# Attention of blocks 4 to 7 in two pairs, each beside merge, selection and gates of the pair ahead

## The chip, the core and the metric

One core of a Trainium2 chip runs the whole program. The metric is device time in microseconds of one execution; three runs of the kernel before gave 3388.62, 3393.28 and 3394.96, median 3393.28. All numbers are float32 unless said otherwise. The engines are TensorE (PE), VectorE (DVE), ScalarE (ACT), GpSimd (POOL) and the queue of SyncE (SP), which issues most of the transfers.

## What is computed

The reference is one layer on 1024 tokens of width 1024:

```
proj = rmsnorm(x, w1) @ w_in                     # 8 groups of columns: q, k, v of two attentions, two gates
o_d  = differential attention, 8 heads, softmax(q1 k1) - lam * softmax(q2 k2), causal by chunks of 64
o_c  = chunk attention, 8 heads, each chunk of 64 sees itself and 8 chunks to the left
h    = x + (sig(g_d) * (o_d @ w_bd) + sig(g_c) * (o_c @ w_bc)) @ w_out
q    = rmsnorm(h, w2) @ wq                       # 8 heads x 2 halves, 128 keys each
       top 16 of each half, top 16 of the 256 sums -> 8 x 16 experts of 16384 per token, weights by softmax
h    = h + sum over the chosen experts  gelu(u[e] . xn) * g * v[e]
y    = rmsnorm(h, final_norm_w)
```

## The kernel before

The tokens are eight blocks of 128. Two ways serve the experts. Blocks 2 to 5 (`DBLK`) go through all 16384 experts as dense matmuls in 128 chunks (`dense_experts`, L681), with the chosen weights laid out as a gate table; blocks 0, 1, 6, 7 (`SBLK`) gather each chosen row by indirect DMA (`experts`, L789): per block 128 gathers from u with a product on VectorE each (L809), then 128 from v with a sum each (L815). Blocks 0 and 1 form projection group 0, blocks 2 to 7 group 1.

The steps around the change are generators that `weave` (L52) runs in turn, so that their instructions are written alternately:

- `attention` (L304): for each of 8 heads and each block the scores of the two maps (L347), a VectorE pass that adds the bias and takes the minimum (L353), exp on ScalarE (L360), the combination of the two maps (L392), transposes, copies and products with V (L366 to L373). Then 4 head pairs of the chunk attention. K, V and Q of a head are loaded when its first block comes (`kv_load`, L311). `diff_end` (L408) writes the reciprocal norms of the heads to DRAM.
- `merge` (L478) of a pair of blocks: the norms come back as a broadcast of 1 MB (L495), then branch products, output product, second norm, query product and the first top 16 (`top16`, L558).
- `choose` (L565), called by `sel`: the second top 16, the expert numbers (through one-hot tiles `ohib`) and the softmax weights of one block. For a dense block it leaves the transposed numbers and weights in `it4` (L629).
- `gates` (L643): for four tokens at a time two one-hot tiles (`o2` on VectorE, L653; `o1` half on ScalarE, L660 and L661, half on VectorE, L663), four small products (L669) and a copy into the staging tile `gst` (L671). After 32 tokens `gst`, 2 MB, is stored to DRAM (L673). A block takes 32 steps.

Before, blocks 4 to 7 went through one attention (`att_rest`, L838), beside merge and selection of blocks 2 and 3. Its outputs were stored to DRAM per head (`ond`, `ocd`) and loaded again per pair (`mop`, L848). Then merge 4, 5 ran beside the gates of blocks 2, 3, and merge 6, 7 beside selection 4, 5 and, after that, the gates of 4, 5. Selection 6, 7 and the dense experts follow, and last in the source stand the gathers.

The order on each engine is laid out when the program is built: a planner walks through the instructions by the order in which they were written and by when its model of their costs says that their inputs are ready, so that what was written late fills gaps. Each engine then runs its list strictly in order. A tile whose place in SBUF belonged to an earlier tile waits until that one is released. Pools are opened and closed as a stack: what `at2` held is free for `gk` only afterwards. The split of a weight tile into two parts (`wtile`, L192; `split`, L126) uses the tags `wh` and `wl` of the pool `wp`, which stands for the whole program.

Of the kernel before, what the change touches and what calls it, by code (L numbers as in the profile page):

```python
# [7 lines left out]
F32 = mybir.dt.float32  # L8
F32R = mybir.dt.float32r
# [6 lines left out]
P = 128  # L16
# [24 lines left out]
JG = 4  # L41
PBUFS = 4
LAG = 1
GLAG = 2
GACT = 2
W1N = 46
HALVES = (slice(0, 64), slice(64, 128))
# [19 lines left out]
def chain(*gens):  # L67
    for g in gens:
        yield from g
# [3 lines left out]
def layer_kernel(ctx, tc, x, w1, w_in, b_gate, lq1, lk1, lq2, lk2, subln, rel,  # L73
# [23 lines left out]
    hd = [drp.tile([P, D], F32, name=f"hd{b}") for b in range(NB)]  # L97
    gdr = [drp.tile([P, NCH, TB], F32, name=f"gdr{i}") for i in range(DT // TB)]
    rst = {}
    ond = [drp.tile([P, 4 * P], F32, name=f"ond{h}") for h in range(H)]  # L100
    ocd = [drp.tile([P, 4 * P], F32, name=f"ocd{h}") for h in range(4)]

    cst = con.tile([P, 3], F32, name="cst")
    for i, c in enumerate((EPS, -0.5 * EPS, 1.5)):
# [46 lines left out]
    def setup():  # L151
# [37 lines left out]
        nc.sync.dma_start(nbias, bass.AP(tensor=tfd.tensor, offset=tfd.offset + 127, ap=[[383, P], [P * 384, H], [1, 256]]))  # L189
        nc.vector.memset(nbias[0:64, :, 192:256], BIG)  # L190

    def wtile(src, K=KC):  # L192
        raw = wp.tile([P, KC, P], F32, name="wr", tag="wr", bufs=WBUFS)[:, :K, :]
        nc.sync.dma_start(raw, src)
        hi = wp.tile([P, KC, P], F32R, name="wh", tag="wh")[:, :K, :]
        lo = wp.tile([P, KC, P], F32R, name="wl", tag="wl")[:, :K, :]
        split(raw, hi, lo)
        return hi, lo

# [12 lines left out]
    def norm1(gi, xp):  # L212

        T = len(GROUPS[gi]) * P
        xh = xp.tile([P, KC, T], F32R, name="xh", tag="xh")
        xl = xp.tile([P, KC, T], F32R, name="xl", tag="xl")
        for i, b in enumerate(GROUPS[gi]):
            xt = wp.tile([P, KC, P], F32, name="xt", tag="wr", bufs=WBUFS).rearrange("p a b -> p (a b)")
            nc.sync.dma_start(xt, x[b * P:(b + 1) * P, :])
            xs = wp.tile([P, KC, P], F32, name="xs", tag="wl").rearrange("p a b -> p (a b)")  # L220
            ss = sm.tile([P, 1], F32, name="ss", tag="ss")
            nc.scalar.activation(xs, xt, AF.Square, accum_out=ss)
            r = rsqrt(sm, ss, 1, 1.0 / D)
            nc.scalar.activation(xs, xt, AF.Copy, scale=r)
            for g in range(2):
                o = transposes([xs[:, (4 * g + j) * P:(4 * g + j + 1) * P] for j in range(4)])
                for j in range(4):
                    c = 4 * g + j
                    oj = o[:, j * P:(j + 1) * P]
                    hi, lo = xh[:, c, i * P:(i + 1) * P], xl[:, c, i * P:(i + 1) * P]  # L230
                    nc.scalar.activation(hi, oj, AF.Copy, scale=w1c[:, c:c + 1])
                    nc.vector.scalar_tensor_tensor(lo, oj, w1c[:, c:c + 1], hi.bitcast(F32), op0=OP.mult, op1=OP.subtract)  # L232
            yield
        dn[gi].x = (xh, xl)
# [330 lines left out]
    def choose(yz, b):  # L565
# [60 lines left out]
        nc.vector.reciprocal(gs, gs)  # L626
        nc.vector.tensor_mul(g, g, gs.unsqueeze(2).to_broadcast([P, H, TK]))
        if b in DBLK:
            it4 = con.tile([P, 4, P], F32, name="it4", tag="it4", bufs=2)  # L629
            t = transposes([sel[:, 0].rearrange("p a b -> p (a b)"), sel[:, 1].rearrange("p a b -> p (a b)"),  # L630
                            g.rearrange("p a b -> p (a b)")])
            nc.scalar.copy(it4[:, 0:3, :], cols4(t, 3))
            nc.scalar.activation(it4[:, 3, :], t[:, 2 * P:3 * P], AF.Copy, scale=-1.0)
            dsel[b] = it4
# [5 lines left out]
            idx_of[b] = (ei, g)  # L640
        yield

    def gates(gk, segs):  # L643

        pend = []
        gst = None
        for k0 in segs:
            it4 = dsel[DBLK[k0]]
            for t in range(0, P, 4):
                if t % TB == 0:  # L650
                    gst = gk.tile([P, NCH, TB], F32, name="gst", tag="gst", bufs=2)
                o2 = gk.tile([P, 4, P], F32, name="o2", tag="o2", bufs=GLAG + 1)
                nc.vector.tensor_tensor(o2, iota.unsqueeze(1).to_broadcast([P, 4, P]),  # L653
                                        it4[:, 1, t:t + 4].unsqueeze(2).to_broadcast([P, 4, P]), op=OP.is_equal)
                o1 = gk.tile([P, 4, P], F32, name="o1", tag="o1", bufs=GLAG + 1)
                for k in range(4):
                    tk = slice(t + k, t + k + 1)
                    if k < GACT:
                        sq = gk.tile([P, P], F32, name="sq", tag="sq", bufs=2)
                        nc.scalar.activation(sq, iota, AF.Square, bias=it4[:, 0, tk], scale=-1.0)  # L660
                        nc.scalar.activation(o1[:, k, :], sq, AF.Relu, bias=it4[:, 2, tk], scale=it4[:, 3, tk])  # L661
                    else:
                        nc.vector.tensor_scalar(o1[:, k, :], iota, it4[:, 0, tk], it4[:, 2, tk],  # L663
                                                op0=OP.is_equal, op1=OP.mult)

                def later(n=k0 * P + t, t=t, o1=o1, o2=o2, gst=gst):
                    o = psp.tile([P, 512], F32, name="gg", tag="tr")
                    for k in range(4):
                        nc.tensor.matmul(o[:, k * P:(k + 1) * P], o2[:, k, :], o1[:, k, :], start=True, stop=True)  # L669
                    tt = t % TB  # L670
                    nc.scalar.copy(gst[:, :, tt:tt + 4].rearrange("p i t -> p t i"), cols4(o, 4))  # L671
                    if tt == TB - 4:
                        nc.sync.dma_start(gdr[n // TB], gst)  # L673
                pend.append(later)
                if len(pend) > GLAG:
                    pend.pop(0)()
                yield
        for f in pend:
            f()

    def dense_experts():  # L681


        T = DT
        with ExitStack() as st:
            dk = st.enter_context(tc.tile_pool(name="dk", bufs=2))
            smd = st.enter_context(tc.tile_pool(name="smd", bufs=2))
            xh = dk.tile([P, KC, T], F32R, name="x2h", bufs=1)
# [67 lines left out]
                    sums(chunks)  # L756
                new = (j, (ah, al), (vh, vl))
            def last(tag, src):
                t = wp.tile([P, KC, P], F32, name="last", tag=tag).rearrange("p a b -> p (a b)")
                nc.sync.dma_start(t, src)  # L760
                return t

# [60 lines left out]
    def outputs(yz, T):  # L823
        return (yz.tile([P, KC, T], F32, name="on", tag="y"), yz.tile([P, 4, T], F32, name="ocx", tag="z"))
# [10 lines left out]
                             lambda h, i, t: nc.scalar.activation(on[:, h, :], t, AF.Copy, scale=sub),  # L835
                             lambda h, i, t: nc.scalar.copy(ocx[:, h, :], t))

    def att_rest(wk):  # L838
        def put(dst, i, t, scale):
            s = wk.tile([P, 2 * P], F32, name="oT", tag="oT")  # L840
            nc.scalar.activation(s, t, AF.Copy, scale=scale)
            nc.sync.dma_start(dst[:, i * P:(i + 2) * P], s)

        yield from attention(wk, S, 1, [4, 5, 6, 7], 2, lambda h: None,
                             lambda h, i, t: put(ond[h], i, t, sub),
                             lambda h, i, t: put(ocd[h], i, t, 1.0))

    def mop(k, mp, yz):  # L848
        on, ocx = outputs(yz, 2 * P)
        cs = slice((k - 2) * 2 * P, (k - 1) * 2 * P)  # L850
        for dst, src in ((on, ond), (ocx, ocd)):
            for h in range(len(src)):
                nc.sync.dma_start(dst[:, h, :], src[h][:, cs])
        yield from merge(mp, 1, [2 * k, 2 * k + 1], yz, on, ocx)

    def sel(blocks, yz):
        for b in sorted(blocks, key=lambda b: b not in DBLK):
            yield from choose(yz, b)
# [5 lines left out]
    def pool(name):  # L864
        return tc.tile_pool(name=name, bufs=1)
# [1 line left out]
    def wpool(name):  # L867
        return tc.tile_pool(name=name, bufs=2)

    with pool("x1") as x1, pool("stp") as stp:  # L870
        dn[1] = Dense(1, stp)
        dn[0] = Dense(0, stp)
        with pool("yz1") as yz1, wpool("at0") as wk:
            with pool("x0") as x0:
                run(norm1(0, x0))
                dn[0].upto(3)
                setup()
                dn[0].upto(6)
                weave(att_one(wk, 0, yza), 13, (dn[0].run(), 46))
            with pool("mp0") as mp:  # L880
                weave(merge(mp, 0, [0], yza, *ons[0]), 25, (att_one(wk, 1, yz1), 13))
                run(sel([0], yza))
                weave(merge(mp, 0, [1], yz1, *ons[1]), 25, (norm1(1, x1), 6))
            run(sel([1], yz1))
        with wpool("at1") as wk:
            dn[1].upto(6)
            weave(att_pair(wk, 1, yza), 25, (dn[1].run(), 46))
    with pool("yzb") as yzb, pool("mp") as mp:
        d1 = [k for k in range(ND) if DBLK[k] < 4]
        d2 = [k for k in range(ND) if DBLK[k] >= 4]  # L890
        with wpool("at2") as wk:
            weave(att_rest(wk), 49, (chain(merge(mp, 1, [2, 3], yza, *ons[1]), sel([2, 3], yza)), W1N))
        with pool("gk") as gk:
            weave(mop(2, mp, yzb), 26, (gates(gk, d1), 32 * len(d1)))
            weave(mop(3, mp, yza), 26, (chain(sel([4, 5], yzb), gates(gk, d2)), 18 + 32 * len(d2)))
    fstack.close()
    run(sel([6, 7], yza))
    dense_experts()
# [53 lines left out]
```

## Time and profile before

| | us |
|---|---|
| runs, median | 3393.28 |
| profiled execution, its own time | 3385.27 |
| span of its profile | 3383.5 |
| TensorE busy | 3101.4 |
| VectorE busy | 2696.5 |
| ScalarE busy | 1445.1 |
| GpSimd busy | 1249.5 |

The span is from the first to the last instruction, and the execution's time lies 2 us above it. Busy times are sums over the whole program; which engine sets the pace differs between its stages, so tables of stretches of the span are what to read. A stretch's row gives the busy time of each engine with its instructions, the mean clock granted to TensorE (1.00 is 2.4 GHz, 0.50 is 1.2 GHz), the busy share of the DMA engines and the bytes per second. A busy TensorE at a lower clock does less. Groups of instructions carry their count, their busy time, the mean of one in ns, and after the second bar the idle time of their engine before them with what ended it.

### The profile page before, as it was taken

Reading aid. Unit: us, or ns where it says so; the run is one execution under the profiler, and the core shown is the slowest. Engines: PE = TensorE matmul, PEld = TensorE weight load, DVE = VectorE, ACT = ScalarE, POOL = GpSimd, SP = SyncE. Lnnn points to the kernel's source line nnn. Section 1 sums busy time; section 2 is a strip of 40 time slices with the busy share of each in tenths; the row PEclk is TensorE's granted clock in tenths of the full one; section 3 lists DMA queues with packets and bytes.
Section 4 is the critical chain, followed back from the end, with each engine's and each line's share of the span. In section 5 each row is a group of like instructions: output and inputs, shape, how many; then the busy total and the mean of one; then the engine's idle time right before and its main releaser. Section 6 shows DMA issues by size and latency. Waiting matters only on the chain.

```text
span 3383.5 us, 48294 instructions
## 1 busy us (share of the span) xinstructions
PE 3101.4 (92%) x16032; PEld 2548.4 (75%) x16032; DVE 2696.5 (80%) x5848; ACT 1445.1 (43%) x3029; POOL 1249.5 (37%) x1028
## 2 busy tenths in 40 slices
PE   7997689999979886987787699999999999999998
PEld 7986578888857664676676578888888888888886
DVE  4436797777769999888885999888888888898843
ACT  5634433434324544567749833333323323322323
POOL 0000455555544532344100035555555555555400
PEclk9998899999989897998898899999999999999999
DMA  7675999999999975898744579999999999999841
GB/s 240 217 243 192 369 323 352 334 355 333 332 340 356 323 269 176 281 325 332 269 152 151 210 265 356 344 336 335 340 335 353 329 335 338 337 343 341 314 128 69
DMA packets 406122, 987.13 MB, mean 292 GB/s; under 512 B 43184, under 2 KB 188400, under 8 KB 403696
## 3 DMA queue, kind: packets, MB, share of 16 engines
q0 software_dynamic: 147456, 536.94, 44.8%
q1 hardware_dynamic: 258416, 447.11, 38.0%
q8 instruction: 126, 2.06, 0.2%
q14 instruction: 124, 1.02, 0.1%
HBM read 905.72 MB, written 78.15 MB: 291 GB/s over the span
## 4 chain that ended last, share of the span: by engine, by line
PE 75%; DVE 12%; DMA 5%; ACT 4%; issue 3%; POOL 1%; SPq 0%; DVEq 0%; POOLq 0%; ACTq 0%
PE ph L136 21%; PE mm L136 17%; PE acc L710 15%; PE mm L490 7%; PE acc L717 5%; PE sc L347 3%; PE pv L372 3%; PE tr L203 2%; DVE junk L809 1%; DMA ge<-in_u_dram,ei 1%; PE gg L669 1%; DVE acc L815 1%; DVE qs L561 1%; DVE iu L563 1%; DVE iu L560 1%
## 5 line engine op out<-in xcount | busy, mean ns | idle before, releaser
L803 POOL DMA_INDIRECT ge<-in_u_dram,ei x512 | 616.7, 1205 | 1258.1 <-DVE junk L809 380.3
L803 POOL DMA_INDIRECT ge<-in_v_dram,ei x512 | 632.6, 1236 | 686.9 <-DVE acc L815 469.3
L815 DVE SCALAR_TENSOR_TENSOR acc<-ge,a,acc 128x1024 f32<-128x1024 f32 x512 | 655.1, 1279 | 21.6 <-DMA ge<-in_v_dram,ei 15.9
L809 DVE SCALAR_TENSOR_TENSOR junk<-ge,xs 128x1024 bf16<-128x1024 f32 x512 | 624.1, 1219 | 50.9 <-DMA ge<-in_u_dram,ei 44.6
L129 DVE TENSOR_TENSOR wl<-wr,wh 128x1024 fp32r<-128x1024 f32 x232 | 283.4, 1222 | 215.8 <-ACT wh L128 110.7
L128 ACT CAST wh<-wr 128x1024 fp32r<-128x1024 f32 x232 | 243.4, 1049 | 404.8 <-PE ph L136 276.5
L136 PE MATMUL ph<-x2h,wh 128*128 128x512 f32 x1024 | 406.2, 397 | 8.8 <-DVE x2l L129 6.6
L136 PE MATMUL ph<-x2l,wh 128*128 128x512 f32 x1024 | 407.7, 398 | 0.0
L136 PE MATMUL mm<-xh,wh 128*128 128x256 f32 (+1 forms) x1248 | 372.1, 325 | 0.7 <-ACT st L286 0.6
L136 PE MATMUL mm<-xl,wh 128*128 128x256 f32 (+1 forms) x1248 | 367.0, 321 | 1.3 <-DVE xl L232 1.2
L136 PE MATMUL ph<-x2h,wl 128*128 128x512 f32 x1024 | 259.4, 395 | 0.0
L136 PEld LDWEIGHTS mm<-xh,wh 128*128 128x128 f32 x1248 | 237.0, 190 | 24.8 <-ACT st L286 3.1
L128 ACT CAST vh<-vr 128x512 fp32r<-128x512 f32 x256 | 140.0, 618 | 269.3 <-PE acc L717 244.5
L136 PEld LDWEIGHTS mm<-xl,wh 128*128 128x128 f32 x1248 | 236.6, 190 | 21.4 <-DVE xl L232 2.0
L136 PEld LDWEIGHTS ph<-x2h,wh 128*128 128x128 f32 x1024 | 193.4, 189 | 55.5 <-DVE x2l L129 7.0
L136 PE MATMUL mm<-xh,wl 128*128 128x256 f32 (+1 forms) x1248 | 234.5, 324 | 0.0
L136 PEld LDWEIGHTS ph<-x2l,wh 128*128 128x128 f32 x1024 | 193.6, 189 | 47.7
L136 PEld LDWEIGHTS ph<-x2h,wl 128*128 128x128 f32 x1024 | 192.0, 188 | 46.9
L347 PE MATMUL sc<-kt,qt 64*128 64x256 f32 (+3 forms) x608 | 200.7, 529 | 14.5 <-DVE mn L353 9.0
L128 ACT CAST ah<-ge 128x512 fp32r<-128x512 f32 x128 | 79.7, 622 | 294.9 <-DVE ge L749 294.9
L710 PE MATMUL acc<-vh,ah 128*128 128x512 f32 x768 | 198.8, 389 | 0.0
L136 PEld LDWEIGHTS mm<-xh,wl 128*128 128x128 f32 x1248 | 184.8, 190 | 16.8
(203 smaller groups left out, 5733.1 us busy)
## 6 DMA issues: line engine op xcount, KB each, us to landing
vr<-in_v_dram SPq DMA_DIRECT2D x128, 512.0 KB, 6.5
wr<-in_ut_dram SPq DMA_DIRECT2D x128, 512.0 KB, 5.8
wr<-in_w_in_dram SPq DMA_DIRECT2D x104, 512.0 KB, 5.3
gdr<-gst SPq DMA_DIRECT2D x16, 2048.0 KB, 8.7
gj<-gdr SPq DMA_DIRECT2D x512, 64.0 KB, 6.0
wr<-in_w_bd_dram SPq DMA_DIRECT2D x40, 512.0 KB, 4.2
wr<-in_w_out_dram SPq DMA_DIRECT2D x40, 512.0 KB, 7.4
wr<-in_wq_dram SPq DMA_DIRECT2D x40, 512.0 KB, 5.1
```

Of the source, the lines that this page charges most:

```text
L128: nc.scalar.copy(hi, raw)
L129: nc.vector.tensor_sub(lo, raw, hi.bitcast(F32))
L136: nc.tensor.matmul(o, w[a][:, k, :], xx[b][:, k, :], start=(i == 0), stop=(i == last))
L203: nc.tensor.transpose(o[:, i * P:(i + 1) * P], s, ident)
L347: nc.tensor.matmul(o[:, :k1 - k0], q, k[:, k0:k1], start=True, stop=True)
L372: nc.tensor.matmul(o[:, :P], aT[:, j - c, :], vt[:, v0 + j, :], start=(j == 0), stop=(j == n - 1))
L490: nc.tensor.matmul(o, w[:, k, :], xx[:, k, :], start=(k == 0), stop=(k == K - 1))
L710: nc.tensor.matmul(acc[i][hf], a[x][:, i * P:(i + 1) * P], b[y][:, hf * 512:hf * 512 + 512], **kw)
L717: nc.tensor.matmul(o, aa[:, 3 * P:4 * P], bb[:, cs], start=(n == 0), stop=(n == len(todo) - 1))
L803: nc.gpsimd.indirect_dma_start(out=t, out_offset=None, in_=src, in_offset=bass.IndirectOffsetOnAxis(ap=ei[:, k:k + 1], axis=0))
L809: nc.vector.scalar_tensor_tensor(junk, t, 1.0, xs, op0=OP.mult, op1=OP.mult, accum_out=hid[:, k:k + 1])
L815: nc.vector.scalar_tensor_tensor(acc, t, a[:, k:k + 1], acc, op0=OP.mult, op1=OP.add)
```

## The change

Blocks 4 to 7 go through two attentions of one pair each (`att_pair`, as blocks 2, 3 did already), whose outputs stay in SBUF. The pair 4, 5 runs beside merge and selection of 2, 3. The pair 6, 7 runs beside merge and selection of 4, 5 and the gates of 2, 3. Merge 6, 7 then runs beside the gates of 4, 5. `gates` takes its number of staging tiles and its lag as arguments: one of each beside attention, two of each after it. `it4` moves to another pool, with four slots. The weights' two parts come from a pool that is open until the projections end (`wf`), and again in the dense stage (`wd`).

```diff
-GLAG = 2
...
-    ond = [drp.tile([P, 4 * P], F32, name=f"ond{h}") for h in range(H)]
-    ocd = [drp.tile([P, 4 * P], F32, name=f"ocd{h}") for h in range(4)]
...
+    parts = []
...
-        hi = wp.tile([P, KC, P], F32R, name="wh", tag="wh")[:, :K, :]
-        lo = wp.tile([P, KC, P], F32R, name="wl", tag="wl")[:, :K, :]
+        hi = parts[-1].tile([P, KC, P], F32R, name="wh", tag="wh")[:, :K, :]
+        lo = parts[-1].tile([P, KC, P], F32R, name="wl", tag="wl")[:, :K, :]
...
-            it4 = con.tile([P, 4, P], F32, name="it4", tag="it4", bufs=2)
+            it4 = fc.tile([P, 4, P], F32, name="it4", tag="it4", bufs=ND)
...
-    def gates(gk, segs):
+    def gates(gk, segs, nst, lag):
...
-                    gst = gk.tile([P, NCH, TB], F32, name="gst", tag="gst", bufs=2)
-                o2 = gk.tile([P, 4, P], F32, name="o2", tag="o2", bufs=GLAG + 1)
+                    gst = gk.tile([P, NCH, TB], F32, name="gst", tag="gst", bufs=nst)
+                o2 = gk.tile([P, 4, P], F32, name="o2", tag="o2", bufs=lag + 1)
...
-                if len(pend) > GLAG:
+                if len(pend) > lag:
...
+            parts.append(st.enter_context(tc.tile_pool(name="wd", bufs=2)))
...
-    with pool("x1") as x1, pool("stp") as stp:
+    with wpool("wf") as wfp, pool("x1") as x1, pool("stp") as stp:
+        parts.append(wfp)
...
         with wpool("at2") as wk:
-            weave(att_rest(wk), 49, (chain(merge(mp, 1, [2, 3], yza, *ons[1]), sel([2, 3], yza)), W1N))
+            weave(att_pair(wk, 2, yzb), 25, (chain(merge(mp, 1, [2, 3], yza, *ons[1]), sel([2, 3], yza)), W1N))
+        with wpool("at3") as wk, pool("gk") as gk:
+            weave(att_pair(wk, 3, yza), 25, (chain(merge(mp, 1, [4, 5], yzb, *ons[2]), sel([4, 5], yzb)), W1N),
+                  (gates(gk, d1, 1, 1), 32 * len(d1)))
         with pool("gk") as gk:
-            weave(mop(2, mp, yzb), 26, (gates(gk, d1), 32 * len(d1)))
-            weave(mop(3, mp, yza), 26, (chain(sel([4, 5], yzb), gates(gk, d2)), 18 + 32 * len(d2)))
+            weave(merge(mp, 1, [6, 7], yza, *ons[3]), 26, (gates(gk, d2, 2, 2), 32 * len(d2)))
```

## Rows read from the trace of the kernel before

**Rows 1.** Stages as a table: stretch, length, busy of each engine (instructions), clock, DMA share, GB/s

```profile
960.00:1477.00 517.00, 443.26 (x2158) 309.22 (x2158) 464.17 (x1353) 227.57 (x557) 203.02 (x190) 0.89 0.84 287
1477.00:1700.00 223.00, 172.82 (x1013) 152.42 (x1014) 197.27 (x545) 164.86 (x381) 66.99 (x54) 0.89 0.82 306
1700.00:1955.00 255.00, 200.51 (x1088) 172.16 (x1087) 200.37 (x845) 185.35 (x423) 0.00 (x0) 0.87 0.51 178
960.00:1955.00 995.00, 816.60 (x4257) 633.80 (x4258) 861.80 (x2741) 577.77 (x1360) 270.01 (x243) 0.88 0.75 263
1955.00:3383.00 1428.00, 1411.19 (x6126) 1150.25 (x6124) 1181.78 (x1592) 448.63 (x688) 648.30 (x512) 1.00 0.87 306
```

**Rows 2.** Instructions of L136: name, count, min/median/max ns, first and last start

```profile
L136 PE MATMUL ph<-x2h,wh x1024: 389/394/796, 1948.1 to 3355.0; 128*128 128x512 f32 x171
```

**Rows 3.** Instructions of L786: name, count, min/median/max ns, first and last start

```profile
L786 DVE SCALAR_TENSOR_TENSOR acc<-acc,nr,wfb x4: 1269/1284/1285, 941.4 to 3211.6; 128x1024 f32<-128x1024 f32 x4
```

**Rows 4.** Stage table for L809 alone (products of the sparse blocks)

```profile
960.00:1477.00 517.00, 144.15 (x236) 0.89 0.84 287
```

**Rows 5.** Stage table for L815 alone (sums of the sparse blocks)

```profile
960.00:1477.00 517.00, 89.16 (x70) 0.89 0.84 287
1477.00:1700.00 223.00, 74.02 (x58) 0.89 0.82 306
1700.00:1955.00 255.00, 0.00 (x0) 0.87 0.51 178
```

**Rows 6.** Chain of waits, 930 to 1960 us: start, us, what

```profile
1453.59 5.16 DMA ocd<-oT
...
1600.05 16.14 DMA rb<-rst
```

**Rows 7.** ScalarE in order of time from 1470 us: start, us, instruction, idle before

```profile
1484.59 0.69 ACT L660 ACTIVATE sq<-iota,it 128x128 f32<-128x128 f32 x2 [6.56 <-DMA ocd<-oT]
```

**Rows 8.** Three more stretches, columns as in the stage table

```profile
1190.00:1360.00 170.00, 134.68 (x595) 89.91 (x593) 165.92 (x655) 72.44 (x178) 48.85 (x49) 0.82 0.67 216
1762.00:1917.00 155.00, 127.13 (x767) 111.19 (x765) 107.82 (x430) 146.16 (x342) 0.00 (x0) 0.90 0.42 157
1917.00:1958.00 41.00, 15.91 (x56) 11.29 (x56) 40.88 (x189) 18.09 (x33) 0.00 (x0) 0.63 0.80 269
```

**Rows 9.** Stage table for L353 alone

```profile
960.00:1955.00 995.00, 110.05 (x384) 0.88 0.75 263
```

**Rows 10.** Groups by line, 960 to 1955 us: count, busy, mean ns, idle before

```profile
L392 DVE SCALAR_TENSOR_TENSOR p<-p,f,p 128x640 f32<-128x640 f32 (+3 forms) x32 | 34.4, 1075 | 0.3
...
L389 DVE RECIPROCAL rz<-z 128x1 f32<-128x1 f32 x32 | 4.9, 153 | 4.3 <-ACT p L360 4.1
```

**Rows 11.** Stretch of selection 4, 5: instructions on cand

```profile
1690.00:1765.00 75.00, 21.20 (x132) 0.88 0.46 148
```

**Rows 12.** Stretch of selection 4, 5: instructions on ohib

```profile
1690.00:1765.00 75.00, 20.10 (x48) 7.31 (x7) 0.88 0.46 148
```

**Rows 13.** Groups by line, 960 to 1955 us, on ScalarE

```profile
L360 ACT ACTIVATE p<-p,mn 128x640 f32<-128x640 f32 (+3 forms) x64 | 63.2, 987 | 98.9 <-DVE mn L353 68.1 <-DMA vt<-vd 29.4 <-DVE rz L390 1.2
L370 ACT COPY aT<-tr 128x512 f32<-128x512 f32 (+3 forms) x128 | 57.8, 463 | 66.9 <-PE tr L203 65.8
...
L360 ACT ACTIVATE pc<-pc,mn 128x640 f32<-128x640 f32 x32 | 26.5, 828 | 8.6 <-DVE mn L353 8.5
```

**Rows 14.** L809 alone from 1190 us

```profile
1190.00:1360.00 170.00, 30.47 (x50) 0.82 0.67 216
```

**Rows 15.** L815 alone from 1190 us

```profile
1190.00:1360.00 170.00, 30.05 (x24) 0.82 0.67 216
```

**Rows 16.** DMA issues: count, KB each, median us to landing

```profile
gdr<-gst SPq DMA_DIRECT2D x16, 2048.0 KB, 8.7
...
rb<-rst SPq DMA_DIRECT2D x3, 1024.0 KB, 16.1
```

**Rows 17.** Groups by line, 960 to 1955 us: split of the first dense weights

```profile
L129 DVE TENSOR_TENSOR wl<-wr,wh 128x1024 fp32r<-128x1024 f32 x2 | 2.4, 1192 | 0.0
```

More of the change, by code (lines that the diff above doesn't have):

```diff
@@ L219, in norm1 @@
             nc.sync.dma_start(xt, x[b * P:(b + 1) * P, :])
-            xs = wp.tile([P, KC, P], F32, name="xs", tag="wl").rearrange("p a b -> p (a b)")
+            xs = parts[-1].tile([P, KC, P], F32, name="xs", tag="wl").rearrange("p a b -> p (a b)")
             ss = sm.tile([P, 1], F32, name="ss", tag="ss")
@@ L650, in gates @@
                 if t % TB == 0:
-                    gst = gk.tile([P, NCH, TB], F32, name="gst", tag="gst", bufs=2)
-                o2 = gk.tile([P, 4, P], F32, name="o2", tag="o2", bufs=GLAG + 1)
+                    gst = gk.tile([P, NCH, TB], F32, name="gst", tag="gst", bufs=nst)
+                o2 = gk.tile([P, 4, P], F32, name="o2", tag="o2", bufs=lag + 1)
                 nc.vector.tensor_tensor(o2, iota.unsqueeze(1).to_broadcast([P, 4, P]),
                                         it4[:, 1, t:t + 4].unsqueeze(2).to_broadcast([P, 4, P]), op=OP.is_equal)
-                o1 = gk.tile([P, 4, P], F32, name="o1", tag="o1", bufs=GLAG + 1)
+                o1 = gk.tile([P, 4, P], F32, name="o1", tag="o1", bufs=lag + 1)
                 for k in range(4):
@@ L758, in last @@
             def last(tag, src):
-                t = wp.tile([P, KC, P], F32, name="last", tag=tag).rearrange("p a b -> p (a b)")
+                t = parts[-1].tile([P, KC, P], F32, name="last", tag=tag).rearrange("p a b -> p (a b)")
                 nc.sync.dma_start(t, src)
@@ L836, in att_pair @@
                              lambda h, i, t: nc.scalar.copy(ocx[:, h, :], t))
[L838 to L854, printed above, removed]
     def sel(blocks, yz):
```

## The prediction

> **What bounds the kernel now.** I read the stage table first [rows 1], because the page's averages mix stages. From 1955 us on TensorE is busy 1411 of 1428 us: the 128 dense-expert chunks run one after another from 1948.1 to 3354.8 us [rows 2], and none of their matmuls changes. The last sparse block is scaled out at 3211.6 us, well before the dense end at about 3380 [rows 3]. So the time is "start of the dense stage" plus a fixed 1428, and the change pays only by what it takes out of 960 to 1955 us, 995 us in which TensorE is busy 817, VectorE 862, ScalarE 578.
>
> That stretch has three stages. A, 960 to 1477: attention of blocks 4 to 7, with merge and selection of 2, 3. B, 1477 to 1700: merge 4, 5 with the gates of 2, 3. C, 1700 to 1955: merge 6, 7, selection 4, 5 and the gates of 4, 5. VectorE is the fullest engine in A and B (464 of 517, 197 of 223), but part of this is filler: the 246 products and sums of the sparse blocks 0 and 1 take 144.2 + 89.2 us of A and 74.0 us of B [rows 4, 5]. They are written last in the source and yet run here, so they sit where VectorE had a gap in the planned order. What the front itself asks of VectorE is 464.2 - 233.4 = 231 in A, 197.3 - 74.0 = 123 in B and 200 in C, 554 us of 995. So no engine is full with the front's own work; the stages lose time to waits and to filler that runs ahead of it.
>
> The chain of waits shows three such places that hang on the order of the stages: 5.16 us for the last store of the attention output, and 16.14 us for the broadcast of the norms [rows 6]; and ScalarE's first gate instruction comes only after the last of these stores, 6.56 us idle [rows 7]: the gate tiles lie where the attention tiles were, so no gate can run beside attention. In C the gates of 4, 5 run at ScalarE's pace, 146 busy of 155 us, and then 41 us pass in which VectorE is full (40.9) and TensorE nearly idle (15.9) until the dense stage rolls [rows 8].
>
> **The change part by part, with costs.** The work of the three stages stays; its division changes to A' (attention 4, 5 + merge and selection 2, 3), B' (attention 6, 7 + merge and selection 4, 5 + gates of 2, 3) and C' (merge 6, 7 + gates of 4, 5).
>
> What moves. Attention's VectorE work is 110.1 us (L353) + 34.4 (L392) + some 20 for four groups of 32 one-column operations like L389's 4.9 = 165 [rows 9, 10]. The pair 6, 7 has 1920 of the 3328 key columns of the distance part and half of the chunk part, so about 56%: 92 us go from A to B'. Selection of 4, 5 writes cand for 21.2 us and ohib for 20.1 us [rows 11, 12]; with its small operations about 45 us go from C to B'. VectorE's own work is then 231 - 92 = 139 in A', 123 + 92 + 45 = 260 in B', 200 - 45 = 155 in C'. ScalarE: the three largest attention groups take 147.5 us [rows 13], 83 for this pair; 56% of all that ScalarE does in A would be 127; I take 110. With some 12 for the selection's casts, B' asks ScalarE for 165 + 110 + 12 = 287 us.
>
> A'. In A VectorE is busy 0.90 of the time and filler takes 0.45 of it, so the front gets 0.45: 139 / 0.447 = 311 us.
>
> B'. Three streams now feed every engine. From below ScalarE: 287 at the 0.94 that it reached in the gates of C is 305 us. From above VectorE: between 1190 and 1360 us attention, top-16 and filler met, VectorE was busy 165.9 of 170, filler took 30.5 + 30.1 of it [rows 8, 14, 15] and the front 0.62; 260 / 0.62 = 419 us. That stretch is the only one with the same mixture, so I stay near it: 390.
>
> C'. Gates 155 and the 41 us behind them as in C [rows 8], and about 19 until the norms' broadcast (16.1 us for 1 MB [rows 16]) and the first outputs of pair 6, 7 are there: 215. Merge 6, 7 lies beside the gates, as it did.
>
> The sum is 311 + 390 + 215 = 916 against 995: -79 us.
>
> At this place the Trainium skill is to be weighed. The row: VectorE has the highest share of all engines in A and B, and in C it is level with TensorE (200.4 and 200.5) [rows 1]. "Perfetto Trace Analysis", section Optimization Strategy, says that interleaving regimes may help where the most-contended engine changes from one to the next. Taken by raw occupancy it hardly changes here, and by that the change would give about what the first rival below gives. I weigh it less because nearly half of VectorE's time in A and B is filler that may run later.
>
> Small parts. Attention outputs go straight into SBUF: 24 stores and 24 loads fall, with the 5 us and 6.6 us waits (in the sum already, as A's end). K and V of earlier blocks are loaded twice: 112 loads on SP's queue in place of 60, so with the 48 gone SP issues 4 more; the DMA share is 0.84 in A and at least as low later, so nothing, or 10 us if the first loads of the pair 6, 7 find no cover, as their tiles lie where the pair 4, 5 had its own. I take 10. The weight parts' pool now opens with the dense stage: its first split (1.19 us on VectorE [rows 17], charged twice for ScalarE's half) can no longer be done early: 2 us, and 0 if it was not early. The one-slot gate staging: ScalarE's first copy of the next 32 tokens must wait until the 2 MB store has landed, 8.7 us [rows 16], and ScalarE works in order, so exps and copies of attention stand behind it, and behind them TensorE. The planned order can put other work in between; each of the 7 refills costs 0 to 16 us (what the 1 MB broadcast took beside the gathers). I take 2 each, 14 in all. Single slots and one less lag for the one-hot tiles cost nothing while attention fills the engines, and lie in B's 0.74 share of ScalarE if it does not. The selected-index tiles move pool, with four slots: no instruction more.
>
> Net: -79 + 10 + 2 + 14 = -53. The profiled execution took 3385.3 us, its span 3383.5, and the median of the runs is 3393.3, 8 above; so 3332 for such an execution, 3340 against the median. I say 3338.
>
> **Rivals.**
> First: VectorE is the bound, and filler keeps its place. All 246 fillers (307 us) and 139 + 260 us in A' and B' at 0.90 busy are 784 us, with C' 999: with the small parts +30. If filler also fits into C', all of 862 at 0.90 is 958, with the small parts -11. So 3382 to 3423, the middle at no change. For it: 0.976 busy from 1190 to 1360. Against it: filler stands last in the source, and none is left after 1700 us [rows 5], 255 us before it would hurt. The section of the Trainium skill named above would have it so.
>
> Second, slower: the single staging slot. The place is the copy into it on ScalarE in B'; the price is the landing under gathers, 16 us, at 7 refills 112 us where I put 14, so -53 + 98 = +45: 3438. It decides from about 10 us a refill on ((53 + 14) / 7). For it: stage B stores 8 times 2 MB at a DMA share of 0.82, with two slots. Against: 8 gate steps stand between two refills, and ScalarE has 0.74 use in B.
>
> Third: filler yields altogether. B' at 305, A' at 280, C' at 205 is 790; with the small parts -179: 3214. TensorE speaks against it: its 817 busy us are at clock 0.88 and would have to fit.
>
> Fourth: the sparse blocks end last. Displaced filler runs after the dense start, where 512 gathers took 1955 to 3211.6, 2.45 us each. The slack is about 168 us, so it decides from 69 displaced; with all of the 136 that A' doesn't take (311 x 0.45 / 1.27 us is 110 of the 246) it is 333 us: 3393 + (333 - 168) - 53 = 3505.
>
> **How the numbers follow.** Forecast 0.56, first 0.18, second 0.14, third 0.07, fourth 0.05. The measurement can't tell changes within 0.2%, 7 us. Faster: 0.55 + 0.06 + 0.03 + 0.07 + 0.02 = 0.73. Slower: 0.07 + 0.10 + 0.02 = 0.19; same 0.08. The likeliest case alone reaches from 3280 (B' at 330) to 3369 (B' at 419). Out to 8 in 10 the range takes in most of the first rival and the upper half of what lies between forecast and third: 3250 to 3408.
>
> **What would show it.** The first dense matmul 45 to 75 us before 1948 and TensorE full from there; gates of 2, 3 beside attention; A' and B' about 311 and 390 us; C' near 215 with ScalarE at its end the pace. The first rival shows as VectorE at 0.95 in B' with all 128 + 118 fillers done before C'; the second as ScalarE waiting for the store into the staging tile, seven times; the fourth as the sparse sums ending after the dense ones. I am wrong if B' exceeds 450 us, or if the dense stage itself grows.

## The result: 32 us slower, and where they went

The changed kernel took 3425.74 us (median of four runs, 3419.79 to 3430.90), the kernel before, on the same chip, 3393.58: ratio 1.0097, 95% interval 1.0073 to 1.0121. I had forecast 3338.

The profiled execution of the changed kernel took 3430.90 us, that of before 3385.27. The first is the slowest of its four runs, the second lies below all four of its kernel, so the traces differ by 45.6 us where the medians differ by 32. These 45.6 split by two rows, the first dense matmul and the last of the same name (lines of a source line: count, min/median/max ns, first and last start; [rows 2] is its twin):

```profile
L133 PE MATMUL ph<-x2h,wh x1024: 388/389/792, 2014.5 to 3400.6; 128*128 128x512 f32 x171
```

The dense stage starts at 2014.5 instead of 1948.1, 66.4 us later, and takes 1386.1 instead of 1406.9 us, 20.8 less. The stage table, against [rows 1] (A', B', C', all three, dense; columns as there):

```profile
960.00:1340.00 380.00, 293.97 (x1318) 214.42 (x1319) 332.87 (x1033) 129.13 (x328) 164.40 (x144) 0.81 0.86 296
1340.00:1778.00 438.00, 362.58 (x1845) 274.55 (x1844) 369.22 (x1053) 269.29 (x625) 111.58 (x99) 0.86 0.68 238
1778.00:2014.00 236.00, 186.16 (x1080) 163.04 (x1078) 154.20 (x607) 178.26 (x406) 0.00 (x0) 0.87 0.54 193
960.00:2014.00 1054.00, 842.72 (x4238) 652.01 (x4238) 856.29 (x2692) 576.68 (x1359) 275.99 (x243) 0.85 0.71 249
2014.00:3429.00 1415.00, 1396.72 (x6144) 1156.15 (x6144) 1191.24 (x1642) 452.75 (x696) 648.30 (x512) 0.99 0.87 310
```

A' took 380 where I had 311, B' 438 for 390, C' 236 for 215. I count everything from the end of the projections to the first dense matmul as "the front": 988 us before, 1054 after. The row of all three stages in [rows 1] runs 7 us into the dense stage; the front of before alone is

```profile
960.00:1948.00 988.00, 809.67 (x4237) 628.27 (x4237) 854.80 (x2706) 575.28 (x1353) 270.01 (x243) 0.89 0.75 263
```

The work in it is unchanged: 4238 matmul instructions against 4237, 856 us of VectorE against 855. But TensorE is busy 843 us instead of 810, at a granted clock of 0.85 instead of 0.89, and idle 211 instead of 178.

Part of these 66 us is scatter between executions. The dense stage gives back 21 us and the medians lie 32 apart, so by the medians the front grew by 53. Four other profiles with the old order and all its filler (below: the pool alone, the two shifts, the lag of one) have fronts of 996 to 1004 us, and the changed kernel with a lag of two has 1045.

The filler has kept its place: first its products, against [rows 4], then its sums, against [rows 5]. None is left for C':

```profile
960.00:1340.00 380.00, 144.59 (x236) 0.81 0.86 296
```

```profile
960.00:1340.00 380.00, 32.27 (x26) 0.81 0.86 296
1340.00:1778.00 438.00, 131.34 (x103) 0.86 0.68 238
1778.00:2014.00 236.00, 0.00 (x0) 0.87 0.54 193
```

How it hurts can be read at the seam between the two attentions, where the selection of blocks 2, 3, the last of the chunk part and some branch products of a merge feed TensorE. First the stretch, then TensorE in order of time (start, us, instruction, idle before), VectorE at the same place, and two instructions of ScalarE:

```profile
1190.00:1340.00 150.00, 104.45 (x443) 71.53 (x444) 146.77 (x496) 61.29 (x153) 63.66 (x56) 0.71 0.72 236
```

```profile
1316.32 1.38 PE L372 MATMUL pv<-vt,aT 128*128 128x128 f32 x10 [1.09 <-ACT och L451]
1325.60 0.48 PE L203 MATMUL tr<-ident,sel 128*128 128x128 f32 x1 [7.90 <-DVE sel L619]
1325.87 1.06 PE L203 MATMUL tr<-ident,pc 128*128 128x128 f32 x4
...
1354.94 3.32 PE L347 MATMUL sc<-kt,qt 64*128 64x512 f32 x6 [8.99 <-DMA qt<-qd]
```

```profile
1317.47 0.69 DVE L612 TENSOR_TENSOR ohib<-pos,iotaj 128x1024 bf16<-128x1024 bf16 x1
1318.07 1.28 DVE L816 SCALAR_TENSOR_TENSOR acc<-ge,a,acc 128x1024 f32<-128x1024 f32 x1
1319.27 0.69 DVE L614 TENSOR_TENSOR ohib<-ohib 128x1024 bf16<-128x1024 bf16 x1
1319.87 1.28 DVE L816 SCALAR_TENSOR_TENSOR acc<-ge,a,acc 128x1024 f32<-128x1024 f32 x1
1321.06 0.42 DVE L617 TENSOR_TENSOR ohib<-ohib 128x512 bf16<-128x512 bf16 x1
1321.40 1.28 DVE L816 SCALAR_TENSOR_TENSOR acc<-ge,a,acc 128x1024 f32<-128x1024 f32 x1
1322.59 0.29 DVE L617 TENSOR_TENSOR ohib<-ohib 128x256 bf16<-128x256 bf16 x1
1322.79 1.28 DVE L816 SCALAR_TENSOR_TENSOR acc<-ge,a,acc 128x1024 f32<-128x1024 f32 x1
1323.99 0.22 DVE L617 TENSOR_TENSOR ohib<-ohib 128x128 bf16<-128x128 bf16 x1
1324.12 1.28 DVE L816 SCALAR_TENSOR_TENSOR acc<-ge,a,acc 128x1024 f32<-128x1024 f32 x1
1325.32 0.22 DVE L619 TENSOR_TENSOR sel<-ohib 128x64 f32<-128x64 bf16 x1
```

```profile
1315.86 0.20 ACT L360 ACTIVATION_READ_ACCUMULATOR pc<-pc,mn 128x1 f32 x1
...
1325.63 1.04 ACT L611 CAST ohib<-iu 128x1024 bf16<-128x1024 uint32 x1 [7.58 <-DVE sel L619]
```

Between any two links of the selection's chain VectorE runs one filler of 1.28 us. Five of them lie inside TensorE's 7.90 us of waiting for `sel`. VectorE looks full (147 of 150 us), while TensorE is busy 104 of 150 at a clock of 0.71. Attention work is still left there: ScalarE had finished the last probabilities `pc` at 1316.06, before its own wait of 7.58 us for the same `sel`. But their transpositions stand behind that of `sel` in TensorE's list, and they run at 1325.87 without a wait of their own. The last outputs of this attention come after them, and only then, from 1337.99 on, are the K, V and Q of the pair 6, 7 loaded.

In the whole front TensorE waits for `sel` as follows (us in total, times, longest): first in the changed kernel, then in the same without the filler, then with thin filler, both described below. In the kernel before it has no such wait.

```profile
PE tr L203 <- DVE sel L619: 21.5, 4, 11.9
```

```profile
PE tr L203 <- DVE sel L619: 1.0, 1, 1.0
```

```profile
PE tr L203 <- DVE sel L619: 1.2, 1, 1.2
```

### The profile page after: what moved, and what is told of

Read it like the earlier page. It is cut to its first block, busy times and chain, and to the rows that moved or that the text cites. A ratio compares the mean times of both kernels' runs of the same rounds, so it can differ in the third digit from the quotient of the medians.

```text
span 3429.1 us, 48221 instructions
## 1 busy us (share of the span) xinstructions
PE 3109.5 (91%) x16033; PEld 2574.6 (75%) x16033; DVE 2700.8 (79%) x5850; ACT 1447.4 (42%) x3037; POOL 1254.3 (37%) x1028
## 4 chain that ended last, share of the span: by engine, by line
PE 74%; DVE 11%; DMA 7%; ACT 4%; issue 3%; POOL 1%; SPq 0%; DVEq 0%; ACTq 0%; POOLq 0%
PE ph L133 20%; PE mm L133 17%; PE acc L711 15%; PE mm L490 7%; PE acc L718 5%; PE sc L347 3%; PE pv L372 3%; PE tr L203 2%; PE gg L669 2%; DVE junk L810 2%; DMA ge<-in_u_dram,ei 1%; DMA ge<-in_v_dram,ei 1%; DMA gdr<-gst 1%; DMA qt<-qd 1%; DVE iu L560 1%
## 5 line engine op out<-in xcount | busy, mean ns | idle before, releaser
L133 PE MATMUL ph<-x2l,wh 128*128 128x512 f32 x1024 | 400.8, 391 | 0.0
L347 PE MATMUL sc<-kt,qt 64*128 64x512 f32 (+3 forms) x608 | 204.6, 544 | 34.1 <-DVE mn L353 16.1
```

What stands on the lines that cost most here:

```text
L133: nc.tensor.matmul(o, w[a][:, k, :], xx[b][:, k, :], start=(i == 0), stop=(i == last))
L347: nc.tensor.matmul(o[:, :k1 - k0], q, k[:, k0:k1], start=True, stop=True)
```

## The experiments

Ratios are against the kernel before, timed on the same chip at the same time.

**The pool alone.** The kernel before, with the weights' two parts in a pool that is open in the projections and again in the dense stage; the order as it was.

```diff
-        hi = wp.tile([P, KC, P], F32R, name="wh", tag="wh")[:, :K, :]
+        hi = parts[-1].tile([P, KC, P], F32R, name="wh", tag="wh")[:, :K, :]
...
```

> The kernel before with one part of the change alone: the pool of the weights' two parts (open for the projections and again in the dense stage). Theory of placement: the dense products that use these parts start every 227 ns as in the changed kernel, not every 233; 24 of them in each of 128 chunks are 24 x 128 x 0.0067 = 20 us less, front unchanged: about 3373. Rival: the pace comes from something else that the change moved; then no difference within 7 us, 233 ns, perhaps 2 us more for the first split.

3372.21 us, ratio 0.9925 (0.9911 to 0.9938). The dense stage takes 1386 us here too, so the 21 us come from the pool, none from the order:

```profile
L136 PE MATMUL ph<-x2h,wh x1024: 389/389/796, 1957.1 to 3343.5; 128*128 128x512 f32 x171
```

**No filler.** Sparse blocks 0 and 1 left out of each kernel.

```diff
-    for b in SBLK:
+    for b in SBLK[2:]:
```

> The kernel before without the sparse blocks 0 and 1 (their 512 gathers, products and sums and the output of these 256 tokens are left out). It shows the front without filler on VectorE and in the transfers. Filler theory: the 307 us of filler between 960 and 1955 are in the way by a third or more, so that stretch shrinks from 988 us (end of the projections to the first dense product) to about 880. Order theory (the front waits for its own chain of stages): it shrinks by less than 50.

> The changed kernel without the sparse blocks 0 and 1 (same part left out). Filler theory: with filler gone the three streams fill the engines as forecast, and the stretch from the end of the projections to the first dense product, 1054 us, falls to or below that of the kernel before without filler (about 880 or less). Order theory: it stays 40 to 70 us longer than that of the kernel before without filler, because the attention of 6, 7 begins only after the selection of 2, 3 and merge 6, 7 only after that attention.

3276.82 and 3261.20 us, one run each (the projections end 22 us earlier, too, which the fronts leave out). The stages of the old order, then of the new (columns as above):

```profile
938.00:1380.00 442.00, 402.58 (x2083) 282.01 (x2084) 256.07 (x1040) 218.59 (x544) 0.00 (x0) 0.94 0.34 109
1380.00:1570.00 190.00, 170.81 (x1035) 151.81 (x1033) 113.15 (x398) 153.81 (x365) 0.00 (x0) 0.95 0.53 189
1570.00:1841.00 271.00, 203.15 (x1125) 174.70 (x1123) 212.58 (x917) 193.01 (x436) 0.00 (x0) 0.86 0.50 176
938.00:1841.00 903.00, 776.53 (x4238) 608.51 (x4238) 581.80 (x2353) 565.41 (x1343) 0.00 (x0) 0.92 0.42 146
```

```profile
937.00:1247.00 310.00, 274.06 (x1367) 202.19 (x1368) 182.54 (x800) 129.57 (x336) 0.00 (x0) 0.92 0.41 135
1247.00:1610.00 363.00, 320.41 (x1774) 243.43 (x1773) 241.27 (x920) 256.51 (x598) 0.00 (x0) 0.93 0.36 126
1610.00:1847.00 237.00, 187.56 (x1102) 164.67 (x1100) 152.85 (x602) 181.04 (x414) 0.00 (x0) 0.88 0.52 190
937.00:1847.00 910.00, 782.03 (x4239) 610.29 (x4239) 576.65 (x2321) 567.13 (x1347) 0.00 (x0) 0.91 0.42 146
```

The fronts are 903 and 910 us: the filler costs the old order 85 and the new one 145, and without it the new order is still 7 us longer, not 79 shorter. TensorE is the fullest engine of A, B, A' and B' alike (0.91, 0.90, 0.88, 0.88 of them). Of the 145 us, 61 are TensorE's own busy time (843 against 782, at a clock of 0.85 against 0.91), the rest its idle time; of the 85 in the old order, 33 are busy time (810 against 777, at 0.89 against 0.92) and 52 idle time. These are differences of single profiles; by the scatter above, the 60 us between the two costs may be 47.

**Thin filler.** All gathers, but product and sum of blocks 0 and 1 over 64 of 1024 columns.

```diff
+        W = 64 if b < 2 else D
...
-            nc.vector.scalar_tensor_tensor(acc, t, a[:, k:k + 1], acc, op0=OP.mult, op1=OP.add)
+            nc.vector.scalar_tensor_tensor(acc[:, :W], t[:, :W], a[:, k:k + 1], acc[:, :W], op0=OP.mult, op1=OP.add)
```

> The kernel before, with all 512 gathers of the sparse blocks 0 and 1 as they are, but product and sum on VectorE over 64 of 1024 columns (so their outputs are incomplete). It separates what the filler takes on VectorE from what its gathers take from the DMA queues. If the 85 us that the filler cost the old order is VectorE time, the front from the end of the projections to the first dense matmul falls from 988 us to 903 to 920, the execution to about 3310. If it is DMA traffic that delays the loads of attention and merge, the front stays within 15 us of 988, the execution near 3390.

> The changed kernel with the same cut: all gathers, product and sum over 64 of 1024 columns for the sparse blocks 0 and 1. The filler cost this order 145 us. VectorE time: the front falls from 1054 us to 910 to 930, the execution to about 3280, below that of the old order with the same cut by about 15 to 25 (the dense stage's 21, less the order's 7). DMA traffic: the front stays within 20 us of 1054, the execution near 3420. If only the difference between the orders (60 us) is DMA, the front comes to about 970.

3341.99 and 3337.13 us, one run each; the fronts, old and new order:

```profile
961.00:1904.00 943.00, 792.92 (x4237) 621.12 (x4237) 626.01 (x2697) 570.74 (x1353) 230.78 (x238) 0.89 0.76 274
```

```profile
958.00:1924.00 966.00, 794.87 (x4239) 616.87 (x4239) 625.49 (x2686) 575.72 (x1359) 230.88 (x238) 0.90 0.74 270
```

The thin filler is not gone from VectorE. In the old order it still takes 61.6 us there, where the whole filler takes 307; in the new one it is 61.8 of 308. The row is VectorE's work on the gathered tiles, old order:

```profile
961.00:1904.00 943.00, 61.62 (x356) 0.00 (x0) 230.78 (x238) 0.89 0.76 274
```

Neither theory holds alone. Time on VectorE is at least 45 of the old order's 85 us and at least 88 of the new one's 145; the 40 and 56 that are left belong to the gathers and to this last fifth of the time on VectorE, which the runs don't separate. The difference between the orders is 66 us with the filler, 23 with thin filler, 7 without. So at least 43 of the 60 us that the filler costs the new order more are VectorE time.

**One pool for both attentions**, so that the second need not wait until the tiles of the first are released.

```diff
-        with wpool("at2") as wk:
+        with wpool("at2") as wk, pool("gk") as gk:
             weave(att_pair(wk, 2, yzb), 25, (chain(merge(mp, 1, [2, 3], yza, *ons[1]), sel([2, 3], yza)), W1N))
-        with wpool("at3") as wk, pool("gk") as gk:
```

> The changed kernel with one attention pool, opened once for both pairs with the gate pool beside it, so that K, V and Q of the pair 6, 7 need not wait until the pair 4, 5 has let go of its tiles. Order theory, boundary of the pools: the hole of 53 us between the last distance step of 4, 5's chunks (1316) and the first step of 6, 7 (1369) closes, 30 to 50 us less: about 3385. Order theory, selection: what holds the pair 6, 7 is that its outputs take the place of the selection's tiles of 2, 3; then 10 us less at most. Filler theory: no change within 10 us.

3408.99 us, ratio 1.0035 (1.0024 to 1.0046). The front is 1037 us: the seam's pool boundary is worth 17 us there, 17 by the medians and 21 by the ratios, which is none of the three values that I had expected. The first combination of two maps of pair 6, 7 (L391) comes at 1336 instead of 1369, but TensorE then waits for the selection all the same (27.9 us for `sel` in this front). The rest stays.

**Gates out of the attention.** The gates of 2, 3 moved behind the second attention, to those of 4, 5.

```diff
...
-                  (gates(gk, d1, 1, 1), 32 * len(d1)))
...
-            weave(merge(mp, 1, [6, 7], yza, *ons[3]), 26, (gates(gk, d2, 2, 2), 32 * len(d2)))
+            weave(merge(mp, 1, [6, 7], yza, *ons[3]), 26, (gates(gk, d1 + d2, 2, 2), 32 * len(d1 + d2)))
```

> The changed kernel with the gates of blocks 2 and 3 taken out of the second attention and put behind it, with those of 4 and 5, beside merge 6, 7 (two staging tiles, lag 2). If gates woven into attention cost the front time through their waits (staging tile, ScalarE in order), this is faster than the changed kernel: the second attention falls from 438 us to below 340, the last stage grows from 236 us to about 330, and the execution comes to 3405 to 3415. If weaving the gates is sound and the loss lies in the first of the two attentions and in the filler, the last stage grows by the 155 us that 64 gate steps took alone and the attention falls only by some 80 to 110: the execution is 3465 to 3500, slower than the changed kernel by 45 to 80.

3447.41 us, ratio 1.0147 (1.0122 to 1.0171), between the two. From the first combination of two maps of pair 6, 7 (L391) on, at 1369 in the changed kernel and at 1364 here; first the changed kernel's attention, whose last stage is C' above, then both stages of this run:

```profile
1369.00:1778.00 409.00, 342.58 (x1785) 261.87 (x1784) 351.62 (x1015) 263.39 (x614) 102.68 (x91) 0.87 0.66 232
```

```profile
1364.00:1690.00 326.00, 277.03 (x1314) 201.10 (x1315) 287.35 (x843) 136.54 (x319) 107.61 (x93) 0.87 0.71 248
1690.00:2032.00 342.00, 279.10 (x1566) 241.44 (x1564) 237.44 (x849) 313.75 (x720) 0.00 (x0) 0.84 0.45 169
```

The attention gets 83 us shorter (326 for 409), the last stage 106 longer (342 for 236), and the front is 1073 us for 1054. Weaving the gates in is no loss; by ratio and medians it saves 17 to 22 us.

**The small staging.** In the kernel before: one staging tile and a lag of one step; the lag alone; the tile alone. In the changed kernel: a lag of two.

```diff
-GLAG = 2
+GLAG = 1
...
-                    gst = gk.tile([P, NCH, TB], F32, name="gst", tag="gst", bufs=2)
+                    gst = gk.tile([P, NCH, TB], F32, name="gst", tag="gst", bufs=1)
```

```diff
-                  (gates(gk, d1, 1, 1), 32 * len(d1)))
+                  (gates(gk, d1, 1, 2), 32 * len(d1)))
```

> The kernel before with one staging tile in place of two and a lag of one step in place of two in the gates, nothing else: the price of the small staging by itself, at 16 stores in stages B and C. My term was 2 us a refill: +14 to +30 us, an execution of 3408 to 3424. The rival had 16 us a refill: over 200 us, 3600. If the 1.2% of the chain that the changed kernel shows behind its stores is all there is (about 5 us a refill where the gates are on the path): +30 to +75. If merge covers it all, no change, 3393.

> The kernel before with a lag of one step, two staging tiles: one half of the edit that took 3395 to 3442. If the lag is what costs, +30 to +46: 3425 to 3440. If the staging tile is, +0 to +12: 3393 to 3405.

> The kernel before with one staging tile, lag two: the other half. If the staging tile costs by its landing (25 us of ScalarE's waits in 9 pieces in the run with both), +20 to +46: 3413 to 3440. If the lag is the cost, +0 to +12: 3393 to 3405. Both halves need not add up, since a lag of two also lets ScalarE go on with other steps while the store lands.

> The changed kernel with a lag of two steps in place of one in the gates beside attention, still one staging tile. If the shorter lag lets TensorE's queue wait for the one-hot tiles and for the copy of the step before, the second attention (438 us) loses 10 to 25 and the execution comes to 3400 to 3415. If attention covers it, as I forecast, or if only the single staging tile costs, it stays at 3420 to 3430.

Both: 3441.81 us, 1.0135 (1.0110 to 1.0159), +46 us. Lag: 3398.87, 1.0015 (1.0003 to 1.0027), +3. Tile: 3418.66, 1.0077 (1.0056 to 1.0097), +23. They don't add up: together they cost 20 us more than apart. Lag two in the changed kernel: 3426.40, no change. Waits for the landing of the staged 2 MB (us in total, times, longest): one tile in the old order from 1400 to 2000, and the changed kernel in B':

```profile
ACT gst L671 <- DMA gdr<-gst: 25.8, 14, 5.7
```

```profile
ACT gst L671 <- DMA gdr<-gst: 1.9, 2, 1.6
```

Beside merge alone, where gates set the pace, the small staging costs; beside attention hardly any wait for it shows. What it would gain to have two tiles there was not tried.

**Where the parts lie.** Between the kernel before and the one with the pool alone, the dense stage's tiles have the same addresses but for the weights' parts: they begin at 73312, 77408, 81504 and 85600 bytes of a partition before, each 32 off a multiple of 64, and at 94336, 98432, 102528 and 106624 with the pool, all multiples of 64. The first kernel shifts the weight tiles of the kernel before by 32 bytes, the second shifts the parts in the new pool back by 32. With a second unused tile behind them, in both, the later tiles move by 64:

```diff
     wp = ctx.enter_context(tc.tile_pool(name="wp", bufs=2))
+    nc.vector.memset(wp.tile([P, 8], F32, name="pad", tag="pad", bufs=1), 0.0)
...
```

```diff
             parts.append(st.enter_context(tc.tile_pool(name="wd", bufs=2)))
+            nc.vector.memset(parts[-1].tile([P, 8], F32, name="pad", tag="pad", bufs=1), 0.0)
...
```

> The kernel before with one unused tile of 32 bytes a partition at the start of the pool of the weight tiles and one at its end, so that the weight tiles and their two parts lie 32 bytes higher and the tiles of all later pools 64 bytes higher; no other change. The parts of the dense weights began at 81504, 85600 (wh) and 73312, 77408 (wl) in the kernel before, each 32 more than a multiple of 64; with the pool of their own they begin at 94336 and so on, all multiples of 64, and only there did the matmuls ph follow each other every 0.2267 us in place of 0.2333. If that place is the cause, the dense stage takes 1386 us in place of 1407 here too, without any change of pools, and the execution comes to 3372 or a little below (the merges' weights have shifted as well). If the cause is the pool (its neighbours, its slots, the order of release), the dense stage stays at 1407 and the execution at 3393 to 3395.

> The kernel before with the pool for the weights' parts alone, and in that pool an unused tile of 32 bytes a partition ahead of the parts (and one behind, so that what follows is shifted by 64): the parts of the dense weights lie 32 bytes off a multiple of 64 again, x2h and x2l do not. By the theory of the place, the pace goes back to 0.2333 us and the dense stage to 1407: 3393 to 3402 in place of 3372. By that of the pool: 3372.

3382.57 us, 0.9966 (0.9954 to 0.9978), and 3390.60, 0.9993 (0.9982 to 1.0003); the same row of each:

```profile
L137 PE MATMUL ph<-x2h,wh x1024: 388/392/796, 1962.8 to 3358.1; 128*128 128x512 f32 x171
```

```profile
L136 PE MATMUL ph<-x2h,wh x1024: 392/394/792, 1957.0 to 3365.0; 128*128 128x512 f32 x171
```

The dense stage takes 1395 and 1408 us. Shifted back by 32 bytes, the parts lose the gain in full. Shifted forward without a pool, to multiples of 64 as well, they get 12 of the 21 us: one such matmul starts every 0.2333 us before, 0.2289 here, 0.2266 with the pool (means from 2300 to 2400 us). So the offset is a cause, not the only one; what withholds the other half stays open.

**Filler held back.** The last 56 gathers and sums of block 1 take their indices from a copy that depends on the selection of blocks 6, 7, once in the kernel with the pool alone, once in the changed kernel.

```diff
...
+            nc.vector.scalar_tensor_tensor(late, idx_of[SBLK[3]][0], 0.0, ei, op0=OP.mult, op1=OP.add)
...
-            t = gather(v, k)
+            t = gather(v, k, late if k >= 72 else ei)
```

> The kernel before with the pool for the weights' parts, and the last 56 gathers and sums of the sparse block 1 made to depend on the selection of blocks 6 and 7, so that they run after the dense stage has begun. It tries whether filler can be taken out of the front for good: the sparse blocks end 168 us ahead of the dense ones and a gather after 1955 us takes 2.45, so 56 are 137 us and still fit. At the old order's 85 us for 246 fillers, 56 are 19 us: 3353. If those late fillers lie in gaps, 3372. If the sparse blocks then end last, above 3390.

> The changed kernel with the same 56 gathers and sums held back. At the new order's 145 us for 246 fillers, 56 are 33 us: 3388 in place of 3421. If the last fillers, all in the second attention, are dearer than the mean (B' lost 438 - 363 = 75 us to 103 fillers, 0.73 each), 41 us: 3380. If what was lost hangs on the gap between the two attentions alone, 3415 to 3421.

3345.43 us, 0.9863 (0.9846 to 0.9880), and 3381.61, 0.9966 (0.9952 to 0.9980). Against the same kernels without the hold the ratio falls by 0.62 points (21 us, 0.38 a filler) and by 1.31 (44 us, 0.79 a filler). The first of them, the old order with the pool and the hold, beats both kernels; its sparse blocks now end with the dense ones, so that no more can be held:

```profile
L789 DVE SCALAR_TENSOR_TENSOR acc<-acc,nr,wfb x4: 1279/1284/1285, 938.7 to 3321.8; 128x1024 f32<-128x1024 f32 x4
```

## Why the prediction was wrong

**The step that failed** is the pricing of A' and B' by VectorE: "the front gets 0.45: 139 / 0.447 = 311 us", and for B' 260 / 0.62 and ScalarE's 305 as bounds. It rests on "no engine is full with the front's own work". The work itself I had nearly right: VectorE's own part, without the filler's rows above, is 156 us in A' and 238 in B', together 394 where I had 139 + 260 = 399. What failed is the pace: the front's own work had 0.41 of A' and 0.54 of B', where I had 0.447 and 0.67 (260 of 390). And VectorE was not full, but idle for 47 us of A' and 69 of B'.

Without filler TensorE fills 0.88 to 0.91 of A, B, A' and B' at a clock of 0.92 to 0.95. I had its row (443 of 517, 173 of 223 [rows 1]) and read it as slack, because the gaps and the clock of 0.89 that it has with filler make TensorE look less than full. My 311 and 390 lie near what the new order takes with no filler at all, 310 and 363, but that is chance, since I had counted filler into them; and by the same measure the old order has 85 us less, too. The gain that I forecast is not there: without filler the new order is no shorter than the old one, and with filler it is longer.

The Trainium skill ("Perfetto Trace Analysis", section Optimization Strategy) says that interleaving regimes may help where the most-contended engine changes from one to the next. In the runs without filler it doesn't change between A and B, and the order alone gave nothing (+7 us): so far the trace agrees. In C VectorE is ahead (213 us against TensorE's 203), and the change moved a selection from there, so this run is no full test of the rule. I had set it aside because I took the filler's share for time that the front could have.

**Where the 66 us of the front went.** About 13 are scatter: the medians give 53. The pool of the parts is not behind them, as the shift without a pool has a front of 1000 us. 7 are the order without filler and 17, measured with filler, the pool boundary between the two attentions; the two may overlap. The rest, 42 by the profiles and 29 by the medians, is the filler beside the new order, for the larger part through its time on VectorE. One place of it is measured: TensorE waits 21.5 us for `sel` in the changed kernel, not at all in the old order, and 1.0 us in the new one without filler. In the old order attention still ran beside all of that selection, until its last store at 1478.06 (the one at 1453.59 [rows 6] that I took for it is the last but one). How the remainder divides over other places, the runs don't say.

**The other terms.** C' 215: 236, and 237 without filler. 7.6 us of these 21 are one wait that I had put at nothing: the gate pool is closed and opened again between B' and C', so ScalarE's first gate of blocks 4, 5 waits until the last store of the gates of 2, 3 has landed:

```profile
1796.27 0.69 ACT L660 ACTIVATE sq<-iota,it 128x128 f32<-128x128 f32 x2 [7.56 <-DMA gdr<-gst]
```

First loads of pair 6, 7 at 10 us: 17 by the run with one pool, with TensorE's 8.99 us for `qt` at 1354.94 as the part that is seen. Staging, 14 us: 1.9 us of waiting for the copies in B', and a longer lag gained nothing; two tiles beside attention were not tried, so the whole of this term isn't measured. "A fixed 1428" behind the start: from the first dense matmul to the end of the span it is 1435 us before and 1415 after, by the parts' place, which I had priced only by their first split, at +2 us. Neither of the signs that I had named for being wrong came (B' stayed below 450 us, and the dense stage shrank): I had named none for A', which came out 69 us above its forecast.

**The rivals.** The first came nearest: all fillers ran before C', and it gave 3382 to 3423. At least 88 of the filler's 145 us are time on VectorE, too. But VectorE was at 0.88 and 0.84 in A' and B', not at the 0.95 of its sign; it is no bound that VectorE reached, but waits and a lower clock for TensorE. The second has a true mechanism in the wrong place: 23 us in the old order, and beside attention 1.9 us of waits. The third (3214, filler yields) had a front of 790 us; with no filler at all it is 910. The objection that I wrote beside it, that TensorE's 817 us would have to fit, held against my own forecast as well. The fourth did not occur: the last sparse block is scaled out at 3265.1, the dense stage's last matmul of this name starts at 3400.6.

## What to carry to other kernels

Work that fills gaps makes an engine look full that isn't the bound, and the bound look slack: before pricing a new order, take the filler's gaps and the lower clock out of the busy shares, or measure both orders without it. Filler on an engine that works through its list in order is not free. Here 246 of them cost 85 us in the old order and 145 in the new one, where among other things a chain of short steps on the same engine alternated with them while TensorE stood waiting for the chain's end; what was ready for TensorE stood behind that wait in its list. Holding 56 of them back until the dense stage gained 21 us in the old order and 44 in the new.

## What the hardware showed unexpectedly

The pace of the dense matmuls hangs on where the stationary tiles begin: 0.2333 us a matmul at 32 bytes off a multiple of 64 in both layouts tried, 0.2266 and 0.2289 at multiples of 64 in two others. From 0.2333 to 0.2266 it is 21 us over 3072 matmuls; why the layout with 0.2289 gets only part of it is open. And the price of one staging tile and a short lag is not the sum of both: 23 and 3 us apart, 46 together.
